# Compressed values copied per head with zero rows, the compression's input stored position outermost, and one key set with its low parts last

## The chip, the cores and the metric

The program runs on one core of one Trainium2 chip. A core has five engines, each with its own queue of instructions: TensorE (PE, matrix products; its weight loads are listed apart as PEld), VectorE (DVE), ScalarE (ACT), GpSimd (POOL) and SyncE (SP, which here only issues transfers). They wait for each other through semaphores. The metric is the device time of one execution in microseconds (us); lower is better. TensorE multiplies a stationary operand (at most 128 rows by 128 columns) with a moving operand of up to 512 columns and adds the result up in PSUM; all other data lies in SBUF, on 128 partitions.

## What is computed

One layer of a decoder: a pooling mixer, a sparse attention with three branches (compressed keys, selected blocks, sliding window), a cross-attention into 256 memory tokens, a merge of the three, and a layer of 16384 single-neuron experts. The sequence is 512 tokens, the width 1024, the attention has 16 heads in 4 groups of 4, each of 64 dimensions. The change touches the compressed branch and the first of the memory keys:

```python
CMP_LEN, CMP_STRIDE = 32, 16
n_cmp = (T - CMP_LEN) // CMP_STRIDE + 1            # 31 compressed positions
def compress(tok, pe, w):                          # 32 tokens, plus a position term, times w
    blk = tok[:, tok_idx] + pe[None, None, :, None, :]
    blk = blk.transpose(0, 1, 3, 2, 4).reshape(B, n_cmp, G, CMP_LEN * dh)
    return blk @ w
kc = compress(k_cmp_tok, pe_k, w_cmp_k)
vc = compress(v_cmp_tok, pe_v, w_cmp_v)
...
p_c = masked_softmax(s_c, mask_c) * has[None, None, None, :, None]
o_c = jnp.einsum('bgrqc,bcgd->bqgrd', p_c.astype(vc.dtype), vc)
...
kv = rms_norm(mem, g_mem) @ w_mem_kv               # memory keys and values
```

## The kernel before

Every operand of a large product is split into a high part (`F32R`, a reduced format) and the rest, the low part: `split` (L127 to L129) makes the high part by a copy on ACT and the low part by a subtraction on DVE or POOL. A product is then three: high by high, high by low, low by high. `mm3_steps` (L143) issues them; its flag `lows_last` sets the order of the 24 matmuls of one tile: without it high and low parts of the moving operand alternate under one weight tile, with it all high-by-high come first, then low weights by high, then high weights by low.

The whole program is written out by hand in the order in which it stands on each engine's queue (`manual_schedule`). Weights come through `Feed`: SP fetches a 512 KB tile, ACT and POOL (or DVE) split it, two tiles ahead of their use. The stages, with the times that the trace shows, are these.

1. Head, 0 to 45 us: rows are normalised and transposed; `mem_keys` (L328) makes the memory keys of four heads into `Kh`, `Kl`, from `mh` and `ml`, the normalised memory transposed (high and low).
2. Cross-attention, pooling and compression, 45 to 163 us, in the order that the string `cross_order` (L220) spells. `k0`, `k1`, `v0`, `v1` are calls of `cmp_z` (L536): a projection tile of 24 matmuls lands in PSUM, and four DVE additions (L545) write it, with the position term, into `TP`. `TP` holds, per partition, 4 groups by 31 compressed positions by 16 tokens, the token index innermost. `kc` and `vc` are calls of `cmp_fold` (L549): 16 plain float32 matmuls (L553), one for each token index `l`, whose moving operand is `TP[:, :, :, l]`, 124 columns that lie 16 elements (64 bytes) apart. The trace shows each as two records.
3. Merge of the cross-attention and the first queries, 163 to 247 us. `cmp_rows` (L562) stands inside it: four transposes turn the compressed values, and four calls of `split` write them into `VC`, once for each head `r` of a group at partitions 32r to 32r+30.
4. Attention, 247 to 532 us: 128 units of one head, one branch and one block of 128 queries, woven with projection tiles as filler for PE. `outputs` (L917) adds up one head's output of 256 queries: matmuls of values by transposed probabilities (L923), then, in the second branch, two more for the compressed branch (L929). Those two use 32 rows of the array: weights `VC[rr, gq]` and moving operand `PC[gq, qp][i][rr]`, both partitions 32r to 32r+31, with `tile_position`. `gather_out` (L932) and `add_out` bring the result to SBUF.
5. Output projection, retrieval and the experts, 532 us to the end at 1885.7 us, where PE runs almost without a gap.

PSUM tiles are named by their tag: `z` for projections (two buffers), `S` for scores, `tr` for transposes, `o` for outputs.

Of the kernel before, what the change touches and what calls it, by code (L numbers as in the profile page):

```python
# [10 lines left out]
F32 = mybir.dt.float32  # L11
# [13 lines left out]
KD = 8  # L25
# [6 lines left out]
def f(ap):  # L32
    return ap.bitcast(F32)
# [72 lines left out]
def layer(ctx: ExitStack, tc: tile.TileContext, A: dict, out: bass.AP, dbg=None):  # L106
# [58 lines left out]
    def mm3(*a, **k):  # L165
        drain(mm3_steps(*a, **k))
# [161 lines left out]
    def mem_keys(hx):  # L328
        w = feed.take(("mk", hx))
        p = psum("z", [128, T])  # L330
        mm3(p[:, 0:M], w, (mh, ml), KD)
        split(Kh[:, hx], Kl[:, hx], p[:, 0:M])

    pvs = {}
# [46 lines left out]
    ap_ = sbuf(ast, "ap")  # L381
    V = [ap_.tile([128, NB, 4, 2, 64], F32R, name=f"V{br}") for br in range(2)]
    KC = ap_.tile([128, 4, 2, 32], F32R, name="KC")
    VC = ap_.tile([128, 4, 2, 64], F32R, name="VC")
    has = ap_.tile([128, 1], F32, name="has")
    nc.sync.dma_start(has, A["has"])
    vst = ExitStack()
# [148 lines left out]
    def cmp_z(kv, gp_):  # L536
        cp = C["cp"]
        if gp_ == 0:
            C["TP", kv] = cp.tile([128, 4, 31, 16], F32, tag="TP", name="TP", bufs=2)
        p = ztile(4 + 2 * kv + gp_)  # L540
        for gi in range(2):
            a = gi * 64
            for half in range(2):
                b = half * 64
                v.tensor_tensor(C["TP", kv][b:b + 64, gp_ * 2 + gi],  # L545
                                p[a:a + 64, half * 16:half * 16 + 496].rearrange("p (c l) -> p c l", l=16),
                                C["pe2", kv][a:a + 64, half][:, None, :].to_broadcast([64, 31, 16]), op=OP.add)

    def cmp_fold(kv):  # L549
        cp, wc, TP = C["cp"], C["wc", kv], C["TP", kv]  # L550
        pc = psum("o", [128, 256])
        for l in range(16):
            pe.matmul(pc[:, 0:124], wc[:, l], TP[:, :, :, l], start=l == 0, stop=l == 15)  # L553
        pcv = pc[:, 0:124].rearrange("p (g c) -> p g c", c=31)
        if kv == 0:
            nc.sync.dma_start(C["wc", 1], A["w_cmp"][1])
            split(KC[:, :, 0, 0:31], KC[:, :, 1, 0:31], pcv)
        else:
            C["vt"] = pm.tile([64, 4, 31], F32, name="vt")
            v.tensor_copy(C["vt"], pcv[0:64])  # L560

    def cmp_rows():  # L562
        pt = psum("tr", [128, 4, 128])
        for gi in range(4):
            pe.transpose(pt[0:31, gi, 0:64], C["vt"][:, gi], ident[0:64, 0:64])
        for r in range(4):
            o = 32 * r
            split(VC[o:o + 31, :, 0], VC[o:o + 31, :, 1], pt[0:31, :, 0:64])

    g.memset(f(KC), 0.0)  # L570
    g.memset(f(VC), 0.0)
    for c in cross_order:
        n = int(c[1]) if c[1:].isdigit() else None
        if c[0] == "Z":
            cross_q(n)
        elif c[0] == "S":
            cross_scores(n)
        elif c[0] == "R":
            cross_scale(n)
        elif c[0] == "W":  # L580
            wv_part(n)
        elif c[0] == "T":
            cross_turn(n)
        elif c[0] == "O":
            cross_out(n)
        elif c[0] == "P":
            pool_window(n)
            if n == 0:
                gfeed.fetch(1)
                gfeed.part(1)  # L590
        elif c == "A":
            feed.fetch(feed.i + 2)
            feed.part(feed.i + 2)
        elif c == "G3":
            pass
        elif c[0] == "G":
            pool_group(n)
        elif len(c) == 3:
            br, b = int(c[1]), int(c[2])
            values(br, b)  # L600
            if (br, b) == (1, 3):
                vst.close()
                v.tensor_scalar(gsig, gsig, 0.5, 0.5, op0=OP.mult, op1=OP.add)
                v.tensor_scalar(gsig[:, 0, 0:16], gsig[:, 0, 0:16], has, None, op0=OP.mult)
                cmp_open()
        elif c == "kc":
            cmp_fold(0)
        elif c == "vc":
            cmp_fold(1)
        else:  # L610
            cmp_z(int(c[0] == "v"), n)
# [256 lines left out]
    def attention():  # L868
# [48 lines left out]
        def outputs(gq, qp, r, br):  # L917
            if br == 0:
                OP_[r] = psum("o", [128, 256])
            o = OP_[r]  # L920
            for i in range(2):
                for kb in range(2 * qp + 2):
                    pe.matmul(o, V[br][:, kb, gq], PT[br, i][:, kb], start=br == 0 and kb == 0 and i == 0,  # L923
                              stop=False, skip_group_check=True)
            if br == 0:
                return
            rr = slice(32 * r, 32 * r + 32)
            for i in range(2):
                pe.matmul(o, VC[rr, gq], PC[gq, qp][i][rr], start=False, stop=i == 1, tile_position=(32 * r, 0),  # L929
                          skip_group_check=True)  # L930

        def gather_out(gq, qp, r):  # L932
            OT[r] = wk.tile([64, 256], F32, name="ot", bufs=2)
            s.activation(OT[r], OP_[r][64:128], AF.Copy)

        def add_out(gq, qp, r):
            h = gq * 4 + r
# [689 lines left out]
```

## Time and profile before

| | us |
|---|---|
| median of 3 runs | 1889.71 |
| lowest and highest | 1888.18 and 1889.93 |
| the profiled execution, its own time | 1887.47 |
| its span in the trace | 1885.7 |
| PE busy | 1864.7 (99%) |
| DVE, ACT, POOL busy | 1334.6, 836.8, 727.2 |

The span is what the trace covers; the time around it is 1.8 us. Matmuls are pipelined: one record lasts from its first read to its last write, and the next starts long before that, so "busy" does not tell how fast PE works. That is read from the distance between the starts of matmuls that follow each other. A row of the timeline gives the start, the time that the row covers, the engine, the line, the operation, out<-in by the program's names, rows times columns of the array in use, the moving operand's shape, and how many records the row merges.

### The profile page before, as it was taken

Reading aid. Unit: us, or ns where it says so; the run is one execution under the profiler, and the core shown is the slowest. Engines: PE = TensorE matmul, PEld = TensorE weight load, DVE = VectorE, ACT = ScalarE, POOL = GpSimd, SP = SyncE. Lnnn points to the kernel's source line nnn. Section 1 sums busy time; section 2 is a strip of 40 time slices with the busy share of each in tenths; the row PEclk is TensorE's granted clock in tenths of the full one; section 3 lists DMA queues with packets and bytes.
Section 4 is the critical chain, followed back from the end, with each engine's and each line's share of the span. In section 5 each row is a group of like instructions: output and inputs, shape, how many; then the busy total and the mean of one; then the engine's idle time right before and its main releaser. Section 6 shows DMA issues by size and latency. Waiting matters only on the chain.

```text
span 1885.7 us, 28019 instructions
## 1 busy us (share of the span) xinstructions
PE 1864.7 (99%) x10151; PEld 1650.0 (88%) x10151; DVE 1334.6 (71%) x2723; ACT 836.8 (44%) x1437; POOL 727.2 (39%) x568
## 2 busy tenths in 40 slices
PE   8999999999999999999999999999999999999998
PEld 7988888888888888999999999999999999888886
DVE  5353147766534369888996688888888888887786
ACT  6433256766642433464555433333333333333434
POOL 4323454455633233400000455555555555522202
PEclk9999999999999999999999999999999999999999
DMA  5315621111123332455889999989989999999973
GB/s 216 107 59 175 219 84 59 52 54 63 62 79 112 125 112 84 130 170 169 297 287 304 381 381 342 351 325 346 349 325 335 347 344 329 334 353 355 329 276 122
DMA packets 144652, 421.54 MB, mean 224 GB/s; under 512 B 14545, under 2 KB 54225, under 8 KB 141826
## 3 DMA queue, kind: packets, MB, share of 16 engines
q1 hardware_dynamic: 74514, 248.55, 36.6%
q0 software_dynamic: 37024, 134.76, 19.5%
q10 hardware_dynamic: 32976, 36.44, 6.0%
q8 instruction: 80, 1.31, 0.3%
q14 instruction: 58, 0.48, 0.1%
HBM read 381.39 MB, written 43.56 MB: 225 GB/s over the span
## 4 chain that ended last, share of the span: by engine, by line
PE 91%; DVE 6%; ACT 1%; DMA 1%; issue 0%; POOL 0%; SPq 0%; ACTq 0%; DVEq 0%; POOLq 0%
PE z L156 48%; PE S L1477 9%; PE tr L1477 9%; PE o L1477 9%; PE o L923 2%; PE S L880 2%; PE tr L912 2%; PE S L1099 1%; PE o L408 1%; PE o L1334 1%; PE S L1334 1%; PE tr L1334 1%; PE o L553 1%; PE o L929 1%; DVE s L1195 1%; DVE si L1192 1%
## 5 line engine op out<-in xcount | busy, mean ns | idle before, releaser
L128 ACT ACTIVATE wh<-wr 128x1024 fp32r<-128x1024 f32 (+2 forms) x364 | 374.0, 1029 | 221.4 <-issue 71.8
L156 PE MATMUL z<-hfh,wh 128*128 128x384 f32 (+1 forms) x1136 | 395.1, 348 | 0.0
L129 DVE TENSOR_TENSOR wl<-wr,wh 128x1024 fp32r<-128x1024 f32 x254 | 307.2, 1224 | 116.3 <-ACT wh L128 113.8
L156 PE MATMUL z<-hfl,wh 128*128 128x384 f32 (+1 forms) x1136 | 389.2, 343 | 0.0
L129 POOL TENSOR_TENSOR wl<-wr,wh 128x1024 fp32r<-128x1024 f32 (+2 forms) x110 | 241.9, 2200 | 330.8 <-ACT wh L128 269.2
L1347 POOL DMA_INDIRECT ug<-in_v_rows_dram,ids x128 | 178.3, 1393 | 236.1 <-DVE x L1368 216.8
L1347 POOL DMA_INDIRECT ug<-in_u_rows_dram,ids x128 | 192.0, 1500 | 145.9 <-DVE jk L1362 126.7
L156 PE MATMUL z<-hfh,wl 128*128 128x384 f32 (+1 forms) x1136 | 230.3, 344 | 0.0
L156 PEld LDWEIGHTS z<-hfl,wh 128*128 128x128 f32 x1136 | 213.4, 188 | 8.1
L156 PEld LDWEIGHTS z<-hfh,wh 128*128 128x128 f32 x1136 | 213.1, 188 | 7.9 <-ACT wh L128 0.3
L1149 ACT ACTIVATE hg<-z 128x384 f32<-128x384 f32 x128 | 63.0, 492 | 336.2 <-PE z L156 333.9
L156 PEld LDWEIGHTS z<-hfh,wl 128*128 128x128 f32 x1136 | 202.8, 188 | 5.5
L1368 DVE SCALAR_TENSOR_TENSOR x<-ug,wgt,x 128x1024 f32<-128x1024 f32 x128 | 164.0, 1281 | 1.0
L1362 DVE SCALAR_TENSOR_TENSOR jk<-ug,hf 128x1024 f32<-128x1024 f32 x128 | 156.3, 1221 | 1.5
L156 PE MATMUL z<-hnh,wh 128*128 128x512 f32 x384 | 152.1, 396 | 0.0
L156 PE MATMUL z<-hnl,wh 128*128 128x512 f32 x384 | 150.4, 392 | 0.0
L128 ACT ACTIVATE wgh<-gh 128x384 fp32r<-128x384 f32 x128 | 67.3, 525 | 152.0 <-DVE gh L1458 146.6
L901 POOL TENSOR_SCALAR pr<-pr,sm,gsig 128x128 f32<-128x128 f32 (+3 forms) x128 | 78.8, 620 | 88.3 <-DVE sm L959 55.0
L915 DVE TENSOR_TENSOR PB<-tr,PB 128x128 fp32r<-128x128 f32 (+3 forms) x128 | 62.6, 489 | 62.7 <-ACT PB L914 62.2
L129 DVE TENSOR_TENSOR wgl<-gh,wgh 128x384 fp32r<-128x384 f32 x128 | 71.2, 556 | 49.7 <-ACT wgh L128 49.1
L1458 DVE TENSOR_TENSOR gh<-gj,hg 128x384 f32<-128x384 f32 x128 | 72.2, 564 | 39.6 <-ACT hg L1149 37.6
L1535 POOL COPY seen<-gj 128x1 f32<-128x1 f32 x1 | 0.2, 188 | 258.3 <-DMA gj<-gd 258.3
(364 smaller groups left out, 3600.2 us busy)
## 6 DMA issues: line engine op xcount, KB each, us to landing
wr<-in_u_t_dram SPq DMA_DIRECT2D x128, 512.0 KB
wr<-in_v_rows_dram SPq DMA_DIRECT2D x128, 512.0 KB
wr<-in_w_z_dram SPq DMA_DIRECT2D x48, 512.0 KB
gd<-stg ACTq DMA_DIRECT2D x12, 2048.0 KB
gj<-gd SPq DMA_DIRECT2D x16, 1536.0 KB
hd<-hg ACTq DMA_DIRECT2D x56, 192.0 KB
hg<-hd SPq DMA_DIRECT2D x56, 192.0 KB
wr<-in_w_peer_q_dram SPq DMA_DIRECT2D x16, 512.0 KB
```

Source lines behind the costliest of these rows:

```text
L128: s.activation(hi, src, AF.Copy)
L129: (eng or v).tensor_tensor(lo, src, f(hi), op=OP.subtract)
L156: pe.matmul(p, w[a][:, k], xs(x[b], k), start=k == 0 and a == 0 and b == 0, stop=k == nk - 1 and a == 1)
L901: g.tensor_scalar(pr[:, 0:n], pr[:, 0:n], sm, gsig[:, qb, c:c + 1], op0=OP.mult, op1=OP.mult)
L915: return lambda: v.tensor_tensor(lo, pt[:, 0:qb + 1], f(hi), op=OP.subtract)
L1149: s.activation(hg, p[:, 0:NT], AF.Gelu)
L1334: pe.matmul(pg[:, n], oa[:, t_ // 2, :, t_ % 2], ob[:, r, t_ // 2, :, t_ % 2], start=n == 0 and r == 0, stop=n == 3 and r == 1, skip_group ...
L1347: g.indirect_dma_start(out=row, out_offset=None, in_=src, in_offset=bass.IndirectOffsetOnAxis(ap=ids[:, b, k:k + 1], axis=0))
L1362: v.scalar_tensor_tensor(jk, rows.pop(m), 1.0, hf[:, b], op0=OP.mult, op1=OP.mult, accum_out=act[:, m:m + 1])
L1368: v.scalar_tensor_tensor(x1[:, b], rows.pop(m), wgt[:, m - 128:m - 127], x1[:, b], op0=OP.mult, op1=OP.add)
L1458: v.tensor_tensor(gh.rearrange("p (g t) -> p g t", t=UT), G[m // 8][:, :, m % 8 // 2, :, m % 2], H.pop(m).rearrange("p (g t) -> p g t", t= ...
L1477: pe.matmul(acc_o[2 * b + half], a[:, b * 128:(b + 1) * 128], c[:, half], start=k == 0 and i == 0, stop=k == 127 and i == 2)
```

## The change

Three edits, independent of each other.

The compressed values: `cmp_rows` now stores each group once, in `VC[32*gq ...]`, and a new tile `VH` of 128 rows by 4 heads is cleared once. `head_values(gq, r)` copies the 32 rows of group `gq` into `VH` at the 32 partitions of head `r`, so that in `VH[:, r]` all other rows are zero. The two matmuls of `outputs` take all 128 rows of `VH[:, r]` and of the probabilities, without a tile position. The copies for group 0 stand in `cmp_rows`, those for the next group behind `gather_out` of the second half of the queries. `OT` has one buffer instead of two.

The compression: `TP` is stored with the token index outermost. The DVE additions write 16 runs of 31 elements and read PSUM 16 elements apart; the matmul's moving operand is `TP[:, l]`, 124 elements in a row.

The memory keys of head 0 are made with `lows_last`.

```diff
-        mm3(p[:, 0:M], w, (mh, ml), KD)
+        mm3(p[:, 0:M], w, (mh, ml), KD, lows_last=hx == 0)
...
-    VC = ap_.tile([128, 4, 2, 64], F32R, name="VC")
+    VC = ap_.tile([128, 2, 64], F32R, name="VC")
+    VH = ap_.tile([128, 4, 2, 64], F32R, name="VH")
...
-            C["TP", kv] = cp.tile([128, 4, 31, 16], F32, tag="TP", name="TP", bufs=2)
+            C["TP", kv] = cp.tile([128, 16, 4, 31], F32, tag="TP", name="TP", bufs=2)
...
-                v.tensor_tensor(C["TP", kv][b:b + 64, gp_ * 2 + gi],
-                                p[a:a + 64, half * 16:half * 16 + 496].rearrange("p (c l) -> p c l", l=16),
-                                C["pe2", kv][a:a + 64, half][:, None, :].to_broadcast([64, 31, 16]), op=OP.add)
+                v.tensor_tensor(C["TP", kv][b:b + 64, :, gp_ * 2 + gi],
+                                p[a:a + 64, half * 16:half * 16 + 496].rearrange("p (c l) -> p l c", l=16),
+                                C["pe2", kv][a:a + 64, half][:, :, None].to_broadcast([64, 16, 31]), op=OP.add)
...
-            pe.matmul(pc[:, 0:124], wc[:, l], TP[:, :, :, l], start=l == 0, stop=l == 15)
+            pe.matmul(pc[:, 0:124], wc[:, l], TP[:, l], start=l == 0, stop=l == 15)
...
+        for gi in range(4):
+            o = 32 * gi
+            split(VC[o:o + 31, 0], VC[o:o + 31, 1], pt[0:31, gi, 0:64])
         for r in range(4):
-            o = 32 * r
-            split(VC[o:o + 31, :, 0], VC[o:o + 31, :, 1], pt[0:31, :, 0:64])
+            head_values(0, r)
+
+    def head_values(gq, r):
+        s.activation(VH[32 * r:32 * r + 32, r], VC[32 * gq:32 * gq + 32], AF.Copy)
...
+    g.memset(f(VH), 0.0)
...
-            rr = slice(32 * r, 32 * r + 32)
             for i in range(2):
-                pe.matmul(o, VC[rr, gq], PC[gq, qp][i][rr], start=False, stop=i == 1, tile_position=(32 * r, 0),
-                          skip_group_check=True)
+                pe.matmul(o, VH[:, r], PC[gq, qp][i], start=False, stop=i == 1, skip_group_check=True)
...
-            OT[r] = wk.tile([64, 256], F32, name="ot", bufs=2)
+            OT[r] = wk.tile([64, 256], F32, name="ot")
             s.activation(OT[r], OP_[r][64:128], AF.Copy)
+            if qp and gq < 3:
+                head_values(gq + 1, r)
```

What moves on PE's queue in the head, at the first set of memory keys (`mh`, `ml` are the memory's high and low parts, `wh`, `wl` the weights'); before:

```order
L156 MATMUL z<-mh,wh 128x256 [waits Activation_49]
L156 MATMUL z<-ml,wh 128x256 [waits DVE_49]
L156 MATMUL z<-mh,wh 128x256
L156 MATMUL z<-ml,wh 128x256
...
L156 MATMUL z<-mh,wl 128x256 [waits Pool_49]
L156 MATMUL z<-mh,wl 128x256 x7
L187 MATMUL tr<-ident,hb 128x128 [waits DVE_49,PE_49]
```

and now:

```order
L149 MATMUL z<-mh,wh 128x256 [waits Activation_49]
L149 MATMUL z<-mh,wh 128x256 x3
L149 MATMUL z<-mh,wh 128x256 [waits Activation_49]
L149 MATMUL z<-mh,wh 128x256 x3
L149 MATMUL z<-mh,wl 128x256 [waits Pool_49]
L149 MATMUL z<-mh,wl 128x256 x7
L149 MATMUL z<-ml,wh 128x256 [waits DVE_49]
L149 MATMUL z<-ml,wh 128x256 x3
```

The eight products with `ml` have moved from between the high products to behind the eight with `wl`.

On ACT's queue, `cmp_rows` between two weight splits (`wh<-wr`); before:

```order
L128 ACTIVATE wh<-wr 128x1024 [waits DMAHW1_49,Pool_49]
L128 ACTIVATE VC<-tr 31x4x64 [waits PE_49]
L128 ACTIVATE VC<-tr 31x4x64 [waits DVE_49] x3
L128 ACTIVATE wh<-wr 128x1024 [waits DMAHW5_49,Pool_49]
L683 ACTIVATE KK_1682<-z 64x512 [waits DMAHW7_49,PE_49]
```

and now:

```order
L128 ACTIVATE VC<-tr 31x64 [waits PE_49]
L128 ACTIVATE VC<-tr 31x64 [waits DVE_49] x3
L575 ACTIVATE VH<-VC 32x128 [waits Activation_49]
L575 ACTIVATE VH<-VC 32x128 x3
L128 ACTIVATE wh<-wr 128x1024 [waits DMAHW5_49,Pool_49]
```

The four copies out of PSUM are a quarter as wide, and four copies within SBUF stand behind them. In the attention one such copy, without a wait of its own, stands behind 12 of the 32 copies of `ot`, here on ACT's queue between a `PB` copy and an exponential:

```order
L747 ACTIVATE th<-z 128x512
L922 ACTIVATE PB_2289<-tr 128x4x128 [waits PE_49,Activation_49]
L940 ACTIVATE ot<-o 64x256 [waits Activation_49]
L575 ACTIVATE VH<-VC 32x128
L901 ACTIVATE pr,sm<-pr,nm 128x512 [waits DVE_49,Pool_49]
```

No instruction stands between the `ot` copy and the exponential in the kernel before. PE's queue in the attention has the same matmuls in the same places, with `VH` in the place of `VC`.

## Rows read from the trace of the kernel before

**Rows 1.** The page, part 1: busy us, share of the span, instructions

```profile
PE 1864.7 (99%) x10151; PEld 1650.0 (88%) x10151; DVE 1334.6 (71%) x2723; ACT 836.8 (44%) x1437; POOL 727.2 (39%) x568
```

**Rows 2.** PE's groups by line and shape: records, busy us, mean ns of one

```profile
L929 PE MATMUL o<-PcT,VC 32*128 32x256 f32 x64 | 15.9, 327 | 0.0
L553 PE MATMUL o<-TP,wc 128*128 128x124 f32 x64 | 13.8, 387 | 0.0
```

**Rows 3.** Timeline of PE at the attention's end: start us, us covered

```profile
521.38 1.10 PE L923 MATMUL o<-PB,V 128*128 128x256 f32 x8
522.41 0.49 PE L929 MATMUL o<-PcT,VC 32*128 32x256 f32 x2
522.84 0.50 PE L156 MATMUL z<-hnh,wh 128*128 128x512 f32 x1
523.17 0.39 PE L156 MATMUL z<-hnl,wh 128*128 128x512 f32 x1
523.40 0.39 PE L156 MATMUL z<-hnh,wh 128*128 128x512 f32 x1
...
526.49 1.10 PE L923 MATMUL o<-PB,V 128*128 128x256 f32 x8
527.43 0.60 PE L912 MATMUL tr<-ident,pr 128*128 128x128 f32 x4
527.78 2.08 PE L156 MATMUL z<-hnh,wl 128*128 128x512 f32 x8
```

**Rows 4.** Timeline of PE where transposes follow the two 32-row matmuls

```profile
458.77 0.49 PE L929 MATMUL o<-PcT,VC 32*128 32x256 f32 x2
459.19 0.44 PE L912 MATMUL tr<-ident,pr 128*128 128x128 f32 x2
459.38 0.48 PE L880 MATMUL S<-KK,Q 128*128 128x256 f32 x2
```

**Rows 5.** Timeline of PE at the two folds and the bias table

```profile
135.91 6.92 PE L553 MATMUL o<-TP,wc 128*128 128x124 f32 x32
142.48 1.72 PE L481 MATMUL z<-xPT,Vx 128*128 128x512 f32 x6
...
154.93 6.92 PE L553 MATMUL o<-TP,wc 128*128 128x124 f32 x32
161.78 1.03 PE L631 MATMUL z<-oh,rb 32*16 32x512 f32 x2
162.74 0.50 PE L156 MATMUL z<-hnh,wh 128*128 128x512 f32 x1
163.08 0.39 PE L156 MATMUL z<-hnl,wh 128*128 128x512 f32 x1
```

**Rows 6.** Timeline of PE at plain float32 matmuls of the retrieval

```profile
673.26 1.06 PE L1181 MATMUL o<-skt,qT 128*128 128x128 f32 x8
674.07 0.48 PE L156 MATMUL z<-hfh,wh 128*128 128x512 f32 x1
```

**Rows 7.** Two stretches: length, busy us of PE, PEld, DVE, ACT, POOL, granted clock

```profile
123.64:142.48 18.84, 18.84 (x91) 16.62 (x90) 12.09 (x20) 4.35 (x9) 5.71 (x4) 1.00 0.19 56
240.00:535.00 295.00, 292.05 (x1698) 246.39 (x1697) 188.46 (x655) 188.52 (x496) 155.79 (x181) 1.00 0.19 62
```

**Rows 8.** Timeline of the head, all engines but the weight loads

```profile
12.26 0.39 PE L156 MATMUL z<-ml,wh 128*128 128x256 f32 x1 [0.56 <-DVE ml L191]
...
14.26 1.06 ACT L128 ACTIVATE wh<-wr 128x1024 fp32r<-128x1024 f32 x1 [1.16 <-DMA wr<-in_w_mk_dram]
...
15.40 2.40 POOL L129 TENSOR_TENSOR wl<-wr,wh 128x1024 fp32r<-128x1024 f32 x1 [3.15 <-ACT wh L128]
...
17.85 0.86 PE L156 MATMUL z<-mh,wl 128*128 128x256 f32 x5
```

**Rows 9.** Timeline of DVE: the four additions of `k0`

```profile
123.64 2.78 DVE L545 TENSOR_TENSOR TP<-z,pe 64x496 f32<-64x496 f32 x4 [0.89 <-PE z L156]
```

**Rows 10.** ACT's groups by line and shape: the smallest copy within SBUF

```profile
L128 ACT ACTIVATE wh<-wr 128x128 fp32r<-128x128 f32 x4 | 1.2, 312 | 0.0
```

## The prediction

> **What bounds the kernel now.** The first view is the page's table of engines: PE is busy 99% of the span and no other engine over 71% [rows 1]. So a microsecond comes out of the program only if PE spends one less, or if another engine is made so late that PE waits. Since "busy" counts overlapping records, the next view is the distance between starts in the timeline of PE. Its regular pace is 0.117 us for 256 columns of `F32R` (eight L923 from 526.49 to 527.43 are 0.94), 0.23 us for 512 columns (523.17 to 523.40), and 0.11 us from transpose to transpose, (0.60 - 0.27) / 3, with 0.27 for the last one alone [rows 3]. Two groups of PE fall out of that pace: L929, 64 matmuls on 32 rows, and L553, 64 records of 124 columns [rows 2].
>
> **Part A: `VH` for `VC`, 32 pairs of matmuls.** Take the pair at 522.41 [rows 3]. Of the eight L923 before it the last starts at 521.38 + 7 x 0.117 = 522.20, so the step into the pair takes 0.21 us, 0.09 over the pace. The pair itself takes 522.41 to 522.84 = 0.43, where two matmuls of 256 columns on all rows take 0.234: 0.20 over. The first filler matmul behind it takes 0.33 (522.84 to 523.17) where the next takes 0.23: 0.10 over. Sum 0.39 us for one pair. Where transposes follow [rows 4], the step in and the pair cost the same, and the two transposes take 0.19 us (459.19 to 459.38) instead of 0.14 (one gap of 0.11, and 0.03 to the next kind, as 527.43 to 527.78 = 3 x 0.11 + 0.03 has it): 0.34. In the timeline 20 of the 32 pairs are followed by a filler matmul and 12 by transposes or a short score product: 20 x 0.39 + 12 x 0.34 = **11.9 us**. That the cause is the 32 rows and not `VC` or the PSUM tile, another 32-row instruction says, of other data and another tile, L631 [rows 5]: the last L553 starts near 154.93 + 6.92 - 0.39 = 161.46, so the step into L631 is 0.32 where L553's own is 0.21 (0.11 over), and the first filler matmul behind it again takes 0.34 (162.74 to 163.08). On 128 rows the pair is of L923's kind: the same types, the same columns, the same PSUM tile, all rows; I take 0.117 for each. PE's order is unchanged, and the pair's last operand, the probabilities, is written long before.
>
> What A adds: 16 copies of 32x128 on ACT. The nearest row is a copy of 128x128 within SBUF, 312 ns [rows 10]; 12 of them in the attention are 3.7 us on an engine that is busy 188.5 of 295 us [rows 7]. Each stands in front of one exponential, which comes up to 0.31 us later; the scores run four units ahead of their transposes, so this is covered by the lag, and if that cover were gone it would be at most 3.7 us. In `cmp_rows` the four copies out of PSUM shrink to a quarter and four copies come behind them: 0 to 1.2 us for ACT's next weight split, which feeds a tile later than the one that PE is working on; I take 0. One clear more on POOL, ahead of a split that is not needed for another tile, is taken at 0.
>
> What is late next: over 240 to 535 us PE idles 295.00 - 292.05 = 2.95 us [rows 7], waiting for DVE and ACT. PE will now run the same 295 us in 283, while DVE and ACT (188.5 us each) go up to 67%: no engine becomes the bound, but some short waits open. I give back 0.9 us, 8% of the gain; bounds 0 and one half, 6 us. A: **-11.0 us**.
>
> **Part B: contiguous `TP`.** A fold of 32 records lasts from 135.91 until near the next start at 142.48; its records are (6.92 - 0.39) / 31 = 0.211 us apart [rows 5]. The retrieval has the same kind of matmul, plain float32, two records for each product, weights of 128x128, 128 columns that lie in a row, L1181: (1.06 - 0.275) / 7 = 0.112 us apart, and 0.81 us for eight up to the next start [rows 6]. The two differ in the distance between the columns read (64 bytes against 4). With 0.112 in place of 0.211, 32 records save 3.2 us, the two folds 6.3. PE is the engine that is waited for before and behind both folds (it has no idle time from 123.64 to 142.48 [rows 7]), so all of it counts. Bounds: 0 (if the load of the weights, not the stride, sets 0.211) and 6.5; L1181 loads weights of the same size, so I take **-6.3 us**.
>
> What B adds is on DVE: 16 additions that now read PSUM 64 bytes apart. Today one takes 2.78 / 4 = 0.70 us [rows 9]. No row shows DVE reading that far apart. From below 0 (the count of elements is the same; a gain is excluded, since today's reads lie in a row). From above, PE's own loss at that distance, 0.211 - 0.112 over 124 columns = 0.8 ns for each, which over 496 elements would be 0.4 us; or, further, a doubling, 0.70. What that does to the end: the first twelve must be done before `O3` (L481, now at 142.48) gets its PSUM buffer. DVE is busy 12.09 of 18.84 us there [rows 7], which leaves 6.75, less the 3.2 by which PE comes earlier: 3.5 us of cover, 0.3 for each addition. At 0.4 more the price is 12 x 0.4 - 3.5 = 1.3 us, at a doubling 4.9. I take 0: DVE needs an element only every 0.70 / 496 = 1.4 ns, PE a column every 0.9 ns (0.112 / 128), and at 64 bytes PE still gets one every 1.7 ns (0.211 / 124). If that is what the memory gives at such a distance, DVE falls behind by 0.3 ns for an element, 0.15 us for an addition, half of the cover.
>
> The Trainium skill, SBUF — State Buffer, section "Door 1: The DMA port swizzle (why `[64,N]` ≈ `[32,N]`)", has a note that speaks for the one half of B and against the other: a reader that touches a new 16-byte line with each element loses speed in SBUF, and PSUM has lines of 8 bytes, on which patterns that don't lie in a row slow matmuls down. The trace agrees for L553 [rows 5, 6]; for DVE in PSUM no run shows it. By that note the additions would go to the upper end, and the sum would be 4.9 us smaller.
>
> **Part C: the first key set.** PE idles 0.56 us at 12.26 for `ml` [rows 8], and the eight high products now stand in that place: eight of 0.117 us, so up to 0.9 us earlier at the tile's end. But the second key set needs low weights that POOL makes from 15.40 to 17.80, behind ACT's split at 14.26, which waited for the transfer, not for PE; PE takes them at 17.85 [rows 8]. Whatever PE gains it waits for there. C: **0**, bounds 0 and -0.9.
>
> **Sum.** -11.0 - 6.3 = -17.3 us. The profiled execution took 1887.47 us by its own time, so it would take 1870.2. It lies 2.2 us below the median of the three runs, 1889.71; against that median the forecast is **1872.4 us**. What comes behind the attention (PE's experts) has no time of its own that it would wait for, so the gain is carried to the end.
>
> **Rivals.**
>
> 1. The pair costs the same on 128 rows, and A gives nothing: 1872.4 + 11.0 = 1883.4. For it: all 64 records are on 32 rows, and no pair in this trace stands in the same place without them. Against it: L923 beside it, and L631. The Trainium skill, TensorE: Matmul & The Clock Gate, section "🎯 Why this matters for your kernels", states this rule: a matmul with 32 rows takes the time of one with 128, and gains come only from tiles running at once. By that sentence A would be 0; the step of 0.215 against 0.117 [rows 3] speaks against it.
>
> 2. The attention gives half of A back, because DVE and ACT pace it in more places than PE's 2.95 us of idle time show: 1872.4 + 5 = 1877.4. For it: 12 exponentials come later. Against it: both stay at 67%.
>
> 3. The weight load sets the fold's pace, B is 0: 1878.7. Against it: L1181.
>
> 4. Slower: DVE's strided reads. If an addition takes 0.70 + e, the first three groups cost 12 e - 3.5 at `O3`. The fourth is covered by the projection tile behind it (24 x 0.23 = 5.5 us, of which the four take 2.8), so it adds 4 e - 2.7. To lose the 17.3 us and 3.8 more (0.2%), 16 e - 6.2 = 21.1, e = 1.7: the point is an addition of 2.4 us, 3.4 times today's. At four times (2.8 us, e = 2.1) the sum is 27.4 - 17.3 = +10: 1900. For it: no row shows such a read; against it: twice is all that PE loses at this distance. A milder form (e = 0.4 to 0.7) gives 1873.7 to 1877.3.
>
> **How the numbers follow.** Forecast as summed 0.68; half of A given back 0.08; milder form of rival 4 0.08; B nothing 0.06; A nothing 0.05; rival 4 in full 0.02; anything else 0.03. The low end is the full 11.9 and 6.5 with C's 0.9 (1870.4), and 1.5 for the spread of the runs (the lowest of three lay 1.5 under the median): 1869.0. The high end takes in a B of nothing, 1878.7; what it leaves out is rival 1, rival 4 in full and the rest, 0.10. A measurement of this kernel tells about 0.2% from no change, 3.8 us: faster is below 1885.9. The first five cases lie there (0.95); of the last two, 0.05, I put 0.02 on no change and 0.03 on slower. Faster 0.95, the same 0.02, slower 0.03.
>
> **What would show it.** In the profile after: the records of the pair 0.117 apart, the step in and the first matmul behind it at the pace (if the step stays at 0.21, A's cause was another); L553 0.11 apart; L545 still near 0.70 us, and PE without idle time at `T3` and `O3`; PE's idle time from 235 to 520 us under 4 us; the second key set still taking its low weights near 17.85. The forecast is wrong if the folds keep 0.21, if L545 goes past 1.0 us, or if idle time in the attention takes the place of what the pairs save.

## The result, and the profile after

| | before | after |
|---|---|---|
| median, us | 1889.82 of 4 runs | 1873.85 of 4 runs |
| lowest and highest | 1888.18 and 1890.08 | 1873.54 and 1874.12 |
| ratio, 95% interval | | 0.9917 (0.9900 to 0.9934) |
| the profiled execution, its own time | 1887.47 | 1874.12 |

The change takes 16.0 us off the median; the forecast was 17.3. Between the two profiled executions it is 13.35 us. The page of after, part 1, beside [rows 1]: busy us, share of the span, instructions.

```profile
PE 1849.6 (99%) x10151; PEld 1641.8 (88%) x10151; DVE 1333.7 (71%) x2723; ACT 841.9 (45%) x1453; POOL 729.2 (39%) x569
```

The bound is the same. The 16 additional instructions of ACT are the copies, the additional one of POOL is the clear. PE's two groups (line, records, busy us, mean ns of one), beside [rows 2], with ACT's copies:

```profile
L936 PE MATMUL o<-PcT,VH 128*128 128x256 f32 x64 | 12.7, 280 | 0.0
L555 PE MATMUL o<-TP,wc 128*128 128x124 f32 x64 | 7.5, 275 | 0.0
L575 ACT ACTIVATE VH<-VC 32x128 fp32r<-32x128 f32 x16 | 4.9, 308 | 0.4
```

The pair is now of the common kind, and a fold's record is 0.275 us long in place of 0.387. A copy takes 308 ns; the prediction had 312 from a copy of four times the size. The timeline of PE (start us, us covered) at the pair that stands in [rows 3] and at the one in [rows 4] shows what its steps became:

```profile
447.69 0.40 PE L936 MATMUL o<-PcT,VH 128*128 128x256 f32 x2
447.93 0.38 PE L920 MATMUL tr<-ident,pr 128*128 128x128 f32 x2
448.06 0.48 PE L888 MATMUL S<-KK,Q 128*128 128x256 f32 x2
...
507.80 1.10 PE L931 MATMUL o<-PB,V 128*128 128x256 f32 x8
508.75 0.39 PE L936 MATMUL o<-PcT,VH 128*128 128x256 f32 x2
508.97 0.40 PE L156 MATMUL z<-hnh,wh 128*128 128x512 f32 x1
509.21 0.39 PE L156 MATMUL z<-hnl,wh 128*128 128x512 f32 x1
509.44 0.39 PE L156 MATMUL z<-hnh,wh 128*128 128x512 f32 x1
```

From the last L931 (507.80 + 7 x 0.117 = 508.62) the step in is 0.13, the pair 0.22, the first filler matmul 0.24, the next 0.23; the two transposes of the other place take 0.13. All three surcharges of the 32-row pair are gone, at both kinds of place. The folds, and DVE's additions, in the timelines of PE and DVE:

```profile
123.75 2.78 DVE L547 TENSOR_TENSOR TP<-z,pe 64x496 f32<-64x496 f32 x4 [0.89 <-PE z L156]
...
136.02 3.73 PE L555 MATMUL o<-TP,wc 128*128 128x124 f32 x32
139.51 1.64 PE L483 MATMUL z<-xPT,Vx 128*128 128x512 f32 x6
...
151.89 3.73 PE L555 MATMUL o<-TP,wc 128*128 128x124 f32 x32
155.56 1.03 PE L639 MATMUL z<-oh,rb 32*16 32x512 f32 x2
...
659.18 1.05 PE L1189 MATMUL o<-skt,qT 128*128 128x128 f32 x8
```

A fold's records are (3.73 - 0.275) / 31 = 0.111 us apart, and the next matmul starts without a gap. Four additions take 2.78 us, to the hundredth as in [rows 9], though they now read PSUM 64 bytes apart.

Two of these rows serve as milestones for all that follows. Bias table (L631, now L639) and first retrieval product (L1181, now L1189) stood at 161.78 and 673.26 [rows 5, 6] and stand at 155.56 and 659.18: the program is 6.2 us earlier behind the folds and 14.1 behind the attention. So **the stretch between them**, which holds the attention, lasts 511.48 us before and 503.62 after, 7.9 less. The pairs gave 11.9 by their rows; some 4 us were lost again. PE's waits in this stretch (us in total, times, the longest) name the place:

```profile
PEld S L888 <- DVE nm L898: 6.2, 11, 0.9
PE S L888 <- DVE nm L898: 3.5, 8, 0.6
PE o L931 <- ACT PB L922: 1.0, 2, 0.5
```

In the trace of before the first two had 3.3 us in 7 waits and 1.4 us in 3. They are waits of the scores (L888) for a PSUM buffer, which comes free when DVE has taken the maximum of an earlier unit (L898, `nm`). The attention by the same count as in [rows 7] (length, busy us of PE, PEld, DVE, ACT, POOL, granted clock):

```profile
234.00:521.00 287.00, 282.05 (x1698) 243.39 (x1697) 188.73 (x655) 192.82 (x507) 156.58 (x181) 1.00 0.21 63
```

PE idles 287.00 - 282.05 = 4.95 us where it idled 2.95, which is only half of the 4 us. The other half is probably hidden in "busy": a record of 256 columns lasts 0.28 us and the next may start 0.12 behind its start, so up to 0.16 us of a wait leave no idle time (an estimate from these two figures). Counted by starts nothing is hidden. Following the start of every matmul that both kernels share, the losses come at eleven places, 0.1 to 0.56 us each, all between 268 and 383 us, and one of 0.16 at the very end, 3.6 us in all. The table `cuts` gives the first two groups of four heads one tile each of the pooling's output projection as filler, the third two, the last four: the losses lie where filler is thin.

### The profile page after: what moved, and what is told of

Its sections match the earlier page's. It is cut to its first block, busy times and chain, and to the rows that moved or that the text cites. A ratio compares the mean times of both kernels' runs of the same rounds, so it can differ in the third digit from the quotient of the medians.

```text
span 1872.4 us, 28038 instructions
## 1 busy us (share of the span) xinstructions
PE 1849.6 (99%) x10151; PEld 1641.8 (88%) x10151; DVE 1333.7 (71%) x2723; ACT 841.9 (45%) x1453; POOL 729.2 (39%) x569
## 4 chain that ended last, share of the span: by engine, by line
PE 89%; DVE 7%; ACT 2%; DMA 1%; issue 1%; POOL 0%; SPq 0%; ACTq 0%; DVEq 0%; POOLq 0%
PE z L156 47%; PE S L1485 9%; PE tr L1485 9%; PE o L1485 9%; PE o L931 2%; PE S L888 2%; PE tr L920 2%; PE S L1107 1%; PE o L410 1%; PE o L1342 1%; PE S L1342 1%; PE tr L1342 1%; DVE s L1203 1%; DVE si L1200 1%; DVE si L1207 1%; PE z L1107 1%
```

## The experiments

The kernel before was run beside each; its median lay between 1888.4 and 1889.8 us, so times are compared by their ratio, or by the stretch between the two milestones, which a difference elsewhere does not touch. The stretch comes from one profile of each kernel; the kernels that have the attention of before agree in it within 0.1 us, those that have the attention of after within 0.35.

| kernel | median us | ratio to before (95%) | folds' end | stretch |
|---|---|---|---|---|
| before | 1889.82 | | 161.78 | 511.48 |
| after (A, B, C) | 1873.85 | 0.9917 (0.9900 to 0.9934) | 155.56 | 503.62 |
| A alone | 1881.60 | 0.9961 (0.9946 to 0.9975) | 161.69 | 503.36 |
| B alone | 1881.55 | 0.9966 (0.9954 to 0.9979) | 155.00 | 511.43 |
| C alone | 1887.87 | 0.9995 (0.9986 to 1.0004) | 161.61 | 511.51 |
| A and B | 1873.53 | 0.9923 (0.9910 to 0.9937) | 155.34 | 503.28 |
| pair on 32 rows of `VH` | 1882.96 | 0.9971 (0.9960 to 0.9982) | 155.14 | 513.01 |
| pair on 64 rows of `VH` | 1883.12 | 0.9972 (0.9961 to 0.9983) | 155.31 | 512.99 |
| `TP` at 8 and 16 bytes | 1877.06 | 0.9939 (0.9924 to 0.9954) | 158.78 | 503.41 |
| copies on POOL | 1872.08 | 0.9911 (0.9897 to 0.9925) | 155.76 | 501.98 |
| before, one `OT` buffer | 1888.31 | 0.9998 (0.9989 to 1.0007) | 162.28 | 511.52 |
| filler 1, 2, 2, 3 | 1870.34 | 0.9901 (0.9885 to 0.9917) | 155.07 | 500.14 |
| filler 2, 2, 2, 2 | 1868.45 | 0.9892 (0.9876 to 0.9908) | 155.33 | 498.19 |
| filler 2, 2, 2, 2 and copies on POOL | 1867.35 | 0.9884 (0.9867 to 0.9900) | 154.95 | 497.16 |

**The parts, one at a time.** Each takes one edit of the change and leaves the kernel before otherwise as it was. A alone:

```diff
-    VC = ap_.tile([128, 4, 2, 64], F32R, name="VC")
+    VC = ap_.tile([128, 2, 64], F32R, name="VC")
+    VH = ap_.tile([128, 4, 2, 64], F32R, name="VH")
...
-                pe.matmul(o, VC[rr, gq], PC[gq, qp][i][rr], start=False, stop=i == 1, tile_position=(32 * r, 0),
-                          skip_group_check=True)
+                pe.matmul(o, VH[:, r], PC[gq, qp][i], start=False, stop=i == 1, skip_group_check=True)
```

> Part A alone: VH, the pairs on 128 rows, one buffer for OT; the token index stays innermost in TP, and the first key set keeps its order. Theory (the prediction's sum with its give-back): 11.0 us less than before, 1889.8 - 11.0 = 1878.8. Second theory (the trace of the changed kernel: between 235 and 537 us PE gained only 8.0 us of the 11.9, the rest went into waits of PE for score buffers, S L888 <- DVE nm): 1881.8, the pairs' records 0.117 us apart and some 3.5 us of such waits. Rival (the attention's waits come from the earlier start of the attention that B brings): 1877.9, no give-back when B is absent.

Measured 1881.60, 7.4 us below its own before by the ratio; the stretch is 8.1 us shorter, not 11. The second theory holds, and the rival falls: the loss is the same without B (3.8 us against 4.0), so it does not come from the attention's earlier start. PE's row of waits reads as in the kernel with all three parts:

```profile
PE S L888 <- DVE nm L898: 3.6, 8, 0.6
```

B alone:

```diff
-            C["TP", kv] = cp.tile([128, 4, 31, 16], F32, tag="TP", name="TP", bufs=2)
+            C["TP", kv] = cp.tile([128, 16, 4, 31], F32, tag="TP", name="TP", bufs=2)
...
-            pe.matmul(pc[:, 0:124], wc[:, l], TP[:, :, :, l], start=l == 0, stop=l == 15)
+            pe.matmul(pc[:, 0:124], wc[:, l], TP[:, l], start=l == 0, stop=l == 15)
```

> Part B alone: TP with the token index outermost; pairs, VC and the first key set as before. Theory: 6.3 us less, 1889.8 - 6.3 = 1883.5, with the records of the fold 0.112 us apart, the additions of cmp_z at today's 0.67 us, and the whole gain kept through the attention. Rival 1 (contiguous folds only let PE arrive earlier at an attention that DVE and ACT pace): 2 to 3 us of it are lost again in waits of the attention, 1886. Rival 2 (strided reads of DVE cost time that the changed kernel hides elsewhere): additions above 0.8 us.

Measured 1881.55, by the ratio 6.4 us less. The distance from the first fold's start to the bias table falls from 25.87 us (161.78 - 135.91) to 155.00 - 135.46 = 19.54, by 6.33. The stretch keeps its 511.4: nothing is lost in the attention, and rival 1 falls. Its additions (DVE, L545) take 673 ns each against 672: rival 2 falls.

C alone:

```diff
-        mm3(p[:, 0:M], w, (mh, ml), KD)
+        mm3(p[:, 0:M], w, (mh, ml), KD, lows_last=hx == 0)
```

> Part C alone: the first set of memory keys with its low parts last. Theory: 0, 1889.8 +- 1; PE starts the high products some 0.6 to 0.9 us earlier and waits for POOL's low weights at 17.85 us as before. Rival: PE keeps 0.6 to 0.9 us of it, 1889.0, and the second set's low products start before 17.3 us.

The ratio's interval holds no change, and both milestones stand where they stood, within 0.2 us. A and B without C:

```diff
-        mm3(p[:, 0:M], w, (mh, ml), KD, lows_last=hx == 0)
+        mm3(p[:, 0:M], w, (mh, ml), KD)
```

> Parts A and B together, the first key set with alternating parts as before. Theory (C is worth nothing, and A and B add up): 1873.9 with single runs within 0.6 us of each other. Second theory (seen in the runs so far: kernels with C lie within 0.8 us of each other, kernels without it spread over 2.4 to 3.3 us, from the same lowest time on): lowest near 1873.5, median 1874.5 to 1876, a spread of 2 us and more; then C takes away a delay that comes in some executions alone. Rival (A and B do not add up without C): lowest above 1875.

A and B give 1873.53, as much as all three, so C is worth nothing that shows in a median. The single runs did spread, from 1871.95 to 1875.48, as the second theory said, but its median did not come: the lowest lies under every run of the three together. Whether C makes executions more alike is left open; where part of the spread comes from stands in the last section.

**Rows of the array, or the tile?** The copies, `VH` and `OT` stay, the pair goes back to 32 rows, or to the half of the rows that holds the head's:

```diff
+            rr = slice(32 * r, 32 * r + 32)
...
-                pe.matmul(o, VH[:, r], PC[gq, qp][i], start=False, stop=i == 1, skip_group_check=True)
+                pe.matmul(o, VH[rr, r], PC[gq, qp][i][rr], start=False, stop=i == 1, tile_position=(32 * r, 0),
+                          skip_group_check=True)
```

> The whole change, but the pair of the compressed branch takes the 32 rows of VH that hold a head's values, and the same 32 rows of the probabilities, with a tile position, as before; the copies, the single OT buffer, the layout of TP and the order of the first key set stay. Theory (the 32 rows are the price, and copies and OT cost nothing): PE pays the 11.9 us for the pairs again and loses none of it in waits, so 1873.9 + 8.0 = 1881.9, as part B alone; records of a pair 0.215 us apart, and waits for score buffers back at 1.4 us. Rival 1 (the price lay in how VC was laid out or in its age in the buffer, not in the rows): 1873.9. Rival 2 (copies or the single OT buffer cause the attention's waits): waits stay at 3.5 us and the time goes to 1885.

> The same on 64 rows: the pair takes the half of VH that holds a head's values, rows 0 to 63 or 64 to 127, with a tile position. Theory (any step from all rows to a part of them and back costs what 32 rows cost): as on 32 rows, 1881.9, records of a pair 0.21 us apart. Rival 1 (the price grows with the rows left out): about half, 1878. Rival 2 (only 32 rows cost it): 1873.9.

The price is back in full with the new tile, 1882.96, and is the same on 64 rows, 1883.12, in the records as well. PE's group on 32 rows, with the mean ns of one, and a pair with its neighbours in the timeline on 64:

```profile
L937 PE MATMUL o<-PcT,VH 32*128 32x256 f32 x64 | 15.9, 327 | 0.0
```

```profile
516.40 1.10 PE L931 MATMUL o<-PB,V 128*128 128x256 f32 x8
517.44 0.50 PE L937 MATMUL o<-PcT,VH 64*128 64x256 f32 x2
517.86 0.50 PE L156 MATMUL z<-hnh,wh 128*128 128x512 f32 x1
518.20 0.40 PE L156 MATMUL z<-hnl,wh 128*128 128x512 f32 x1
```

From 516.40 + 0.82 the step in is 0.22, the pair 0.42, the first filler matmul 0.34: the numbers of [rows 3]. So it is leaving all rows and coming back that costs, however many are left, and neither `VC` nor its age.

The weight loads (timeline of PEld) show how. Before, at the pair of [rows 3] and the filler behind it:

```profile
522.41 0.29 PEld L929 LDWEIGHTS o<-PcT,VC 32*128 32x128 f32 x2
522.83 0.19 PEld L156 LDWEIGHTS z<-hnh,wh 128*128 128x128 f32 x1
522.94 0.19 PEld L156 LDWEIGHTS z<-hnl,wh 128*128 128x128 f32 x1
```

and after, at the same place:

```profile
508.63 0.31 PEld L936 LDWEIGHTS o<-PcT,VH 128*128 128x128 f32 x2
508.86 0.19 PEld L156 LDWEIGHTS z<-hnh,wh 128*128 128x128 f32 x1
508.98 0.19 PEld L156 LDWEIGHTS z<-hnl,wh 128*128 128x128 f32 x1
```

After, each load starts while the matmul before the one that needs it has only begun: the pair's at 508.63 for 508.75, the filler's at 508.86 for 508.97. Before, the pair's first load starts with the pair itself (522.41), and the filler's with the filler (522.83 for 522.84). It is so at all 32 pairs, and on 32 and 64 rows of `VH` as well. So there are two changes, into the pair and out of it, and each costs twice: the step itself is 0.09 us over the pace, and the distance from the first matmul behind the change to the next is 0.10 over, which is the excess inside the pair and at the first filler matmul. Two times 0.19 is the price of a pair among filler; that the second half of it is the load that found no matmul to run under fits the rows, but no run tests it by itself.

The Trainium skill, TensorEngine Tiling (Array Packing), section "Key Properties", says that a change of the tiling mode drains the engine; these rows agree, and price one such change at 0.2 us. The rule of the Trainium skill behind rival 1 (TensorE: Matmul & The Clock Gate, section "🎯 Why this matters for your kernels"), that a matmul on 32 rows takes the time of one on 128, leaves the change out: the second record of a pair does last 0.27 us, like one on all rows with 0.28, and yet the pair takes 0.43 us against 0.22.

Rival 2 is half right. The pair's price is that of before, and yet the stretch is 513.01 us, 1.5 longer than before's 511.48, and PE's waits for score buffers are 2.0 us against 1.4. So the copies, or the single `OT` buffer, cost 1.5 us by themselves; the theory had them at nothing. The next two kernels part them.

**Copies or `OT`?** The 12 copies in the attention go to POOL:

```diff
-        s.activation(VH[32 * r:32 * r + 32, r], VC[32 * gq:32 * gq + 32], AF.Copy)
+        if gq:
+            g.tensor_copy(VH[32 * r:32 * r + 32, r], VC[32 * gq:32 * gq + 32])
+        else:
+            s.activation(VH[32 * r:32 * r + 32, r], VC[32 * gq:32 * gq + 32], AF.Copy)
```

> The whole change, but the 12 copies of head_values for the groups 1 to 3 run on POOL in place of ACT. On 32 rows with the copies (the run before) PE still lost 1.5 us in the attention that it did not lose with part B alone; part A alone lost 3.6. Theory (those 1.5 us are ACT's copies, which stand ahead of exponentials): they come back, 1873.7 - 1.5 = 1872.2, PE's waits for score buffers fall from 3.5 to some 2 us. Rival 1 (the 1.5 us come from the single OT buffer or from where the reads of OT stand): 1873.7. Rival 2 (a copy on POOL delays a scaling of probabilities or a low part there, for which PE or DVE waits): 1875 or more.

And the kernel before gets one `OT` buffer, nothing else:

```diff
-            OT[r] = wk.tile([64, 256], F32, name="ot", bufs=2)
+            OT[r] = wk.tile([64, 256], F32, name="ot")
```

> The kernel before with one buffer for OT in place of two, nothing else. Theory (it costs nothing, ACT's read of the outputs stands a whole unit behind DVE's addition): 1888.9, attention as before, waits for score buffers 1.4 us. Rival (it is the source of the 1.5 us that the attention loses with copies and OT while pairs stay on 32 rows): 1890.4, waits for score buffers 2 us.

The copies on POOL give 1872.08 and a stretch 1.6 us shorter, as the theory said; PE's waits for score buffers fell less than it said, to 2.9 us; the gain comes at seven places, 0.11 to 0.47 us each, three of them at scores, two at L931, two at filler. Six of the seven are places where the kernel on 32 rows of `VH` had lost about as much against B alone. `OT` costs nothing in the kernel before, ratio 0.9998; with the whole change it was not run by itself, but there too no copy into `ot` waits for the buffer (the trace of after has one wait before these copies, 0.6 us, for PE). How a copy of 0.31 us gets to PE is seen at one place of the timeline of after (ACT, DVE and PE):

```profile
314.68 0.31 ACT L575 ACTIVATE VH<-VC 32x128 fp32r<-32x128 f32 x1
...
315.01 0.51 ACT L901 ACTIVATE pr<-pr,nm 128x256 f32<-128x256 f32 x1
...
315.52 0.40 ACT L808 ACTIVATE cex<-cex 128x256 f32<-128x256 f32 x1
...
315.96 0.42 DVE L812 TENSOR_REDUCE csm<-cex 128x8 f32<-128x256 f32 x1 [1.25 <-ACT cex L808]
...
316.94 0.27 DVE L898 CUSTOM_DVE_ANT_0 pr<-S,TT 128x128 f32<-128x128 f32 x1
...
317.27 0.51 PE L888 MATMUL S<-KK,Q 128*128 128x256 f32 x2 [0.37 <-DVE nm L898]
```

and at the same place with the copies on POOL (its lines are three further on):

```profile
315.17 0.42 DVE L815 TENSOR_REDUCE csm<-cex 128x8 f32<-128x256 f32 x1 [0.78 <-ACT cex L811]
...
316.48 0.50 PE L891 MATMUL S<-KK,Q 128*128 128x256 f32 x2
```

The copy pushes back not only its unit's exponential (L901) but also that of the compressed branch (L808). For that one DVE waits, 1.25 us instead of 0.78, and behind it in DVE's queue stands the maximum L898, on which the next score buffer hangs. PE idles 0.37 us there, and not at all without the copy. The other places were not followed in this way.

**Filler.** What is left of the loss, some 2.4 us (11.9 less the 9.5 by which this last stretch is below 511.48), should then be PE itself, which arrives at a score before DVE is done with an earlier one; so far this is an argument. The table of the filler is changed:

```diff
-    cuts = (0, 1, 2, 4, 8)
+    cuts = (0, 1, 3, 5, 8)
```

> The whole change, and cuts = (0, 1, 3, 5, 8) in place of (0, 1, 2, 4, 8): one more tile of the pooling's output projection (24 matmuls, 7.7 us by the program's own table) stands between the attention units of the second group, one fewer in the last. Theory (the give-back is PE running out of filler while DVE makes the scores' maxima): the waits for score buffers between 305 and 385 us, about 2 us by the trace of the changed kernel, go, none come in the last group, which had none: 1873.9 - 2 = 1872. Rival 1 (these waits are caused by DVE and ACT being late by their own work, which another tile also adds to): no change, 1873.9. Rival 2 (the last group then runs out of filler): 1875 or more.

```diff
-    cuts = (0, 1, 2, 4, 8)
+    cuts = (0, 2, 4, 6, 8)
```

> The whole change with cuts = (0, 2, 4, 6, 8): two filler tiles of the pooling's output projection in each of the four groups (the kernel has 1, 1, 2, 4; the run with 1, 2, 2, 3 took 1870.3). Theory (each group whose PE runs out of filler gains): the first group's waits, between 256 and 312 us 1.1 us of 2.8 in all, go as well, 1869.3. Rival 1 (what is left in the first group are waits for DVE and ACT that filler does not fill): 1870.3. Rival 2 (the last group, with two tiles, now waits in its turn): 1871.5 or more.

One tile earlier in the second group gives 3.5 us by the stretch, more than the waits that the theory counted there; two tiles in every group give 5.4 and a median of 1868.45. The waits of PE for score buffers fell to 2.3 and to 1.2 us, and the attention's busy time of PE in the last of these kernels reads

```profile
234.00:516.00 282.00, 280.37 (x1700) 243.25 (x1699) 188.56 (x656) 193.82 (x509) 156.44 (x181) 1.00 0.21 64
```

1.63 us of idle time in place of 4.95 and of the 2.95 before the change. All rivals of the two kernels fall: DVE and ACT do the same work, and PE waits less for them once it has something else to do, and the last group is not starved by two tiles. In the second kernel the stretch is 13.3 us below before, more than the pairs' 11.9: part of the waits of before must have gone as well, since idle time too is 1.3 us below that of before. The kernel before was not run with this filler, so how much of the 5.4 us is the loss that the change made, and how much it would have gained without the change, is not separated.

Both cures together:

> The whole change with both: two filler tiles in each group, cuts = (0, 2, 4, 6, 8), and the 12 copies on POOL. With one tile more in the first groups the kernel took 1868.45, with the copies on POOL alone 1872.1 in place of 1873.7. Theory 1 (the two are separate losses and add up): 1868.45 - 1.6 = 1866.9. Theory 2 (the filler covers the waits that ACT's copies open, so both cure the same microseconds): 1868.4. Rival (POOL, which splits the filler's weights, is now late for the tiles that stand earlier): 1869 or more.

Measured 1867.35, a stretch 1.0 us shorter than with the filler alone: between the two theories, nearer to the first; the rival falls. Some of the microseconds were the same, most were not. This is 22 us below the kernel before and 6.5 below the changed one.

## Why the prediction was right, and which term was off

**A, the gain of the pairs, right.** 0.39 and 0.34 us for a pair were read as three surcharges, and all three are gone at each kind of place; the trace shows them to be two changes of rows, about 0.2 us each. L631 as a witness for the rows pointed the right way: the same prices on 32 and on 64 rows of `VH`, and none on 128. Rival 1 falls.

**A, the give-back, mis-sized.** The prediction gave back 0.9 us, 8% of the gain, without a row behind it; by the stretch it is 11.9 - 7.9 = 4.0, in A alone 11.9 - 8.1 = 3.8. Its own test, idle time under 4 us, failed with 4.95, and the truth lies in its bounds (0 to 6), nearer to rival 2 than to the term. Two steps failed. One is the cover of the copies, "covered by the lag": the prediction looked at the exponential right behind a copy, while at the place shown the next one on ACT, that of the compressed branch, has DVE waiting, and the maximum behind it in DVE's queue; priced at 3.7 us if the cover were gone, it costs 1.5. The other is to take engines' shares for cover: DVE and ACT stay under 70% of the attention, and yet PE meets a late maximum in the half where filler is thin. This part is some 2.4 us. That earlier filler brings back more than this is shown; that thin filler is all of its cause is argued, from the places of the losses.

**B, right to 0.1 us:** 0.111 for the 0.112, 6.3 us behind the folds. The price of DVE's strided reads, taken at 0 between 0 and 0.70, is 0 (2.78 us for four, before and after), so rival 4 falls in both forms. Rival 3 falls with the folds' 0.111, at weights of the same size.

**C, right.** In the profile after PE starts the second key set earlier (15.40 us against 15.87), and then waits for POOL, as argued:

```profile
17.25 0.28 PE L156 MATMUL z<-ml,wh 128*128 128x256 f32 x1
17.61 1.18 PE L156 MATMUL z<-mh,wl 128*128 128x256 f32 x8
```

0.36 us lie between the last product with high weights and the first with low ones, where the pace is 0.117; the low products come 0.24 us earlier than at 17.85 because POOL's split does, behind a transfer that landed earlier in this execution: ACT's split in front of it starts at 14.02 instead of 14.26 [rows 8]. At the milestones nothing is left of it.

**The sum.** Against its own profiled execution the sum was 1870.2, and the profiled execution after took 1874.12: 3.9 us off, of which 3.1 are the give-back (4.0 - 0.9) and 0.8 lie behind the milestone of the retrieval (1885.7 - 673.26 = 1212.4 us from there to the end, and 1872.4 - 659.18 = 1213.2), in work that the change does not touch. That 0.8 arises between 840 and 1050 us, where the pace described in the last section switches at other times. The median is closer, 1.5 us from the forecast, because the kernel before was profiled in an execution 2.2 us below its median and the one after was not. The two milestones show 14.1 us of gain, and the rest of the 16.0 lies between executions: that the forecast came so near is luck in this part, and with it known the same working would have missed by more.

## What to carry to other kernels

A few matmuls on part of the rows among many on all rows pay at each change, here about 0.2 us on the way in and as much on the way out; in this kernel zero rows were cheaper than the change, and the price is read from the distances of starts around them, not from their own duration. When the busiest engine is made faster, ask of each stage what fills its waits: here a third of the gain went back into waits for another engine's queue, and moving existing filler to that place brought more than that back. A small instruction on a half idle engine is free only if everything behind it in that queue, and in the queue of whoever waits there, has slack.

## What the runs showed of the hardware that was not expected

**Where PE loses its pace.** With `TP` so stored that the columns of a token index lie 8 bytes apart for `kc` and 16 for `vc`:

```diff
-            C["TP", kv] = cp.tile([128, 16, 4, 31], F32, tag="TP", name="TP", bufs=2)
+            C["TP", kv] = cp.tile([128, 16 // li, 4, 31, li], F32, tag="TP", name="TP", bufs=2)
...
-            pe.matmul(pc[:, 0:124], wc[:, l], TP[:, l], start=l == 0, stop=l == 15)
+            pe.matmul(pc[:, 0:124], wc[:, l], TP[:, l // (2, 4)[kv], :, :, l % (2, 4)[kv]], start=l == 0, stop=l == 15)
```

> The whole change with another layout of TP: in the first fold (kc) the columns of one token index lie 8 bytes apart, in the second (vc) 16 bytes; the additions write runs of 2 and of 4 elements. Before it was 64 bytes for both, in the changed kernel 4. Theory (PE loses its pace as soon as the columns do not lie in a row): both folds at 0.211 us from record to record, 1873.9 + 6.3 = 1880.2. Rival 1 (only a distance of 16 bytes and more costs): kc at 0.112, vc at 0.211, 1877.1. Rival 2 (only distances well beyond 16 bytes cost): both 0.112, 1873.9. The Trainium skill, SBUF - State Buffer, section Door 1: The DMA port swizzle, has a note by which a new 16-byte line for each element costs a reader speed; that is rival 1, with something between for the 8 bytes.

```profile
135.75 3.73 PE L555 MATMUL o<-TP,wc 128*128 128x124 f32 x32
139.24 1.64 PE L483 MATMUL z<-xPT,Vx 128*128 128x512 f32 x6
...
151.62 7.23 PE L555 MATMUL o<-TP,wc 128*128 128x124 f32 x32
158.78 1.03 PE L639 MATMUL z<-oh,rb 32*16 32x512 f32 x2
```

Rival 1, with a median of 1877.06; the theory and rival 2 fall. 8 bytes cost nothing, 3.73 us as at 4 bytes; 16 bytes cost as much as 64 and a little more, (7.23 - 0.39) / 31 = 0.221 us for a record where 64 bytes had 0.211 [rows 5]. By the Trainium skill, SBUF — State Buffer, section "Door 1: The DMA port swizzle (why `[64,N]` ≈ `[32,N]`)", two accesses to a line of 16 bytes are needed for full speed; that is this step, and at 8 bytes, where two columns share a line, nothing "between" was lost. The same note's lines of 8 bytes in PSUM, which it tells of matmuls, have no counterpart on DVE here: four additions that read PSUM at 64 bytes took 2.78 us, as those that read it in a row did, and writing runs of 2 and 4 elements (2.78 and 2.73 us in this kernel) or of 31 took no longer either.

**A pace that changes by 2% at a granted clock of 1.00.** Matmuls of 384 columns between 800 and 850 us follow each other by 176.7 ns in the profiles of before and after, and by 173.4 in that of A and B, over some 280 distances each. The windows (columns as above, then the share of DMA and GB/s) of after, and of A and B, show the granted clock and the count of matmuls:

```profile
820.00:850.00 30.00, 30.00 (x173) 29.97 (x172) 26.14 (x41) 14.76 (x17) 0.00 (x0) 1.00 0.53 170
```

```profile
820.00:850.00 30.00, 30.00 (x176) 29.96 (x175) 26.69 (x43) 14.56 (x18) 0.00 (x0) 1.00 0.54 170
```

All the profiles switch from one to the other and back, at times that differ from run to run, from about 770 us on; that of A and B goes to the slower pace only near 890. Followed start by start, this makes 1.6 us between after and the run of A and B at 1871.95, which owes most of its lead to it, and 0.7 us between before and after. What sets it, no run here shows.
